# A four-layer decoder trunk: the angles of the position tables on GpSimd, the small vectors on ScalarE's queue, eleven warming products

## The chip, the cores and the metric

The kernel runs on one core of a Trainium2 chip, as one launch. The metric is device microseconds of an execution, the median of several runs. A profile is one execution taken by the hardware profiler; its span goes from the first to the last instruction.

## What is computed

The reference is a trunk of four pre-norm residual layers over 256 tokens of width 1024 in float32. The token mixers are differential attention (layers 0 and 3), block attention (layer 1) and windowed attention with sinks (layer 2); a squared-ReLU MLP of width 4096 follows each. Every mixer rotates the first quarter of each head's width by angles from the token's position:

```python
def rope_tables(positions):
    inv = ROPE_THETA ** (-jnp.arange(0, ROT_DIM, 2, dtype=jnp.float32) / ROT_DIM)
    ang = positions.astype(jnp.float32)[..., None] * inv
    return jnp.cos(ang), jnp.sin(ang)
...
for i in range(DEPTH):
    a = rms_norm(h, attn_norm_g[i])
    y = ...                                    # mixer i % 3, with cos and sin
    h = h + y
    h = h + sqrelu_mlp(rms_norm(h, mlp_norm_g[i]), mlp_w_up[i], mlp_w_down[i])
return rms_norm(h, final_norm_g)
```

Here 8 angles for each of 256 positions are needed, so the tables are 128 x 16 numbers (128 partitions, two token tiles of 8). They are computed once and used by all four layers.

## The kernel before

**Weights.** All weights are cut on the host into pieces of 128 x 2048 floats (1 MB). Each piece is fetched on SP's queue into `raw` (4 buffers), and split into a high part `whi` (ScalarE, L80) and the rest `wlo` (VectorE, L81). A product of float32 precision is then three TensorE products: high by high, high by low, low by high. `take()` keeps fetches and splits ahead of use: two pieces ahead in conversion, five in fetching. The first two pieces are fetched in quarters of 512 columns that alternate with the eight blocks of `x` (L66, L109), and split quarter by quarter; later pieces are split in halves of 1024.

**Norms.** The activations stay transposed in `hT`. `norm_part` (L228, L229) makes the high and low part of the scaled input, `norm_sum` adds squares, `norm_factor` turns the sums into the factor per token (`rsqrt`, L207 to L211, on VectorE with scratch tiles `nw`). The factor is applied behind the projection, by ScalarE, when it copies `qk` out of the accumulator (L588).

**Projection and attention of layer 0.** `proj` runs 48 matmuls of 512 columns for each of six output parts; the first part goes through the weights in the order in which they arrive. `qk` is rotated by `rope` (L304 to L309, VectorE) with `cc`, `sn` and `nsn`, transposed on TensorE (`p_qk`, L461), split, and scored (`p_s`, L271 to L273). The order of these steps among the projections is a list (`plan`).

**The start.** A memset and an activation on ScalarE come first, then the transfer `gn` (L115): norm gains, sub-norm gains and positions in one tile of 34 KB. GpSimd makes constants and masks. TensorE runs `WARM` products of a tile of ones, which are used by nothing.

**The position tables.** `rotary_tables` is a generator. Up to its `yield` it casts the positions, multiplies by the inverse frequencies and takes off the first multiple of a turn; the rest is run when the first projection has been written down. The angle is reduced modulo whole turns in three rounds: the number of turns is rounded by adding and taking off 12582912, and the turn is taken off in four pieces, so that nothing is lost. Then the angle is clamped, its absolute value is taken (L181 to L184), and ScalarE's Sin gives `sn` and `cc` (L185, L186).

**Order.** The kernel is written in a framework that places semaphores by itself and orders each engine's instructions when the program is built, by priority (what was written first) and its own estimate of when operands are ready. On the chip each engine works its queue in that fixed order. So the order in the trace is not that of the text.

Of the kernel before, what the change touches and what calls it, by code (L numbers as in the profile page):

```python
# [11 lines left out]
F32 = mybir.dt.float32  # L12
# [3 lines left out]
OP = mybir.AluOpType  # L16
AX = mybir.AxisListType

P = 128
D = 1024  # L20
S = 256
NT = S // P
# [5 lines left out]
NEG = -1.0e38  # L28
LOOK = 2
FAR = 5  # L30
WARM = 12
RAW = 4


# [5 lines left out]
def trunk(ctx: ExitStack, tc: tile.TileContext, xT, gains, lams, swa_row, fng, weights, out):  # L40
    nc = tc.nc
    V, A, G, T = nc.vector, nc.scalar, nc.gpsimd, nc.tensor

    cst = ctx.enter_context(tc.tile_pool(name="cst", bufs=1))
    tiny = ctx.enter_context(tc.tile_pool(name="tiny", bufs=2))
# [3 lines left out]
    def bank(tag, name):  # L49
        return ps.tile([P, 512], F32, tag=tag, name=name, bufs=4)  # L50
# [50 lines left out]
    gn = cst.tile([P, 2 * DEPTH * 8 + 2 + NT], F32, name="gn")  # L101
    gv = gn[:, :2 * DEPTH * 8].rearrange("p (k l b) -> p k l b", k=2, l=DEPTH)
    sg = gn[:, 2 * DEPTH * 8:2 * DEPTH * 8 + 2]
    posi = gn[:, 2 * DEPTH * 8 + 2:].bitcast(I32)
# [6 lines left out]

    first_act = cst.tile([P, 1], F32, name="first_act")
    V.memset(first_act, 0.0)
    A.activation(first_act, first_act, AF.Copy)
    nc.sync.dma_start(gn, gains)  # L115
    fetch(4, load_x)
    fetch(4, load_x)
    fetch(2)
# [7 lines left out]
    invt = cst.tile([P, NT, 8], F32, name="invt")  # L126
# [4 lines left out]
    warm = bank("wk", "p_warm")  # L131
    for _ in range(WARM):
        T.matmul(warm[:, :P], ones, ones, start=True, stop=True)
# [18 lines left out]
    def rotary_tables():  # L152

        posf = cst.tile([P, NT], F32, name="posf")
        V.tensor_copy(posf, posi)
        an = cst.tile([P, NT, 8], F32, name="an")
        lo = cst.tile([P, NT, 8], F32, name="an_lo")
        V.tensor_tensor(an, invt, posf[:, :, None].to_broadcast([P, NT, 8]), op=OP.mult)
        G.memset(lo, 0.0)

        for turn, bits in ((2.0 ** 16 * math.pi, 10), (2.0 * math.pi, 9), (2.0 * math.pi, 20)):
            q = cst.tile([P, NT, 8], F32, name="turns")
            V.tensor_scalar(q, an, 1.0 / turn, None, op0=OP.mult)
            V.tensor_scalar(q, q, 12582912.0, None, op0=OP.add)
            V.tensor_scalar(q, q, -12582912.0, None, op0=OP.add)
            for x in (an, an, lo):
                m, e = math.frexp(turn)
                c = math.ldexp(math.floor(m * 2 ** bits), e - bits)
                turn -= c
                V.scalar_tensor_tensor(x, q, -c, x, op0=OP.mult, op1=OP.add)  # L170
            if bits == 10:
                yield
            V.scalar_tensor_tensor(lo, q, -turn, lo, op0=OP.mult, op1=OP.add)
            if bits != 20:
                V.tensor_tensor(q, an, lo, op=OP.add)
                V.tensor_tensor(an, an, q, op=OP.subtract)
                V.tensor_tensor(lo, an, lo, op=OP.add)
                V.tensor_copy(an, q)
        V.tensor_tensor(an, an, lo, op=OP.add)
        pi = 3.1415925  # L180
        V.tensor_scalar(an, an, pi, -pi, op0=OP.min, op1=OP.max)  # L181
        ab = cst.tile([P, NT, 8], F32, name="ab")
        V.scalar_tensor_tensor(ab, an, -1.0, an, op0=OP.mult, op1=OP.max)
        V.tensor_scalar(ab, ab, -1.0, math.pi / 2, op0=OP.mult, op1=OP.add)  # L184
        A.activation(sn, an, AF.Sin)  # L185
        A.activation(cc[:, :, 0:8], ab, AF.Sin)  # L186
        V.tensor_copy(cc[:, :, 8:16], cc[:, :, 0:8])
        V.tensor_scalar(nsn, sn, -1.0, None, op0=OP.mult)
# [14 lines left out]

    def rsqrt(y, x, n):

        t = tiny.tile([P, n], F32, tag="nw", name="nw", bufs=7)
        V.tensor_scalar(y.bitcast(I32), x.bitcast(I32), -0.5, 1597463007.0, op0=OP.mult, op1=OP.add)  # L207
        for _ in range(3):
            V.tensor_tensor(t, y, y, op=OP.mult)
            V.scalar_tensor_tensor(t, t, -0.5, x, op0=OP.mult, op1=OP.mult)  # L210
            V.scalar_tensor_tensor(y, t, 1.5, y, op0=OP.add, op1=OP.mult)  # L211
# [483 lines left out]
    def down_out(us, res, factor):  # L695

        grow = sb.tile([P, D], F32, tag="raw", name="grow", bufs=RAW)
        nc.sync.dma_start(grow, bcast(fng, D))
        ss = cst.tile([P, 4, NT], F32, name="fss")
        x = cst.tile([P, 2, NT], F32, name="fx")  # L700
        r = cst.tile([P, NT], F32, name="fr")

        def close(t, p, c, part, first=0):

            width = p.shape[-1]
            y = res[t][:, 512 * c + first:512 * c + first + width]
            V.scalar_tensor_tensor(y, p, factor[:, t:t + 1], y, op0=OP.mult, op1=OP.add)
            if part is not None:
                sq = sb.tile([P, 512], F32, tag="relu", name="sq")
                A.activation(sq[:, :width], y, AF.Square, accum_out=ss[:, part, t:t + 1])  # L710

        def finish(t, halves):

            o = slice(t, t + 1)
            last = x[:, 1, o]
            V.scalar_tensor_tensor(last, ss[:, halves, o], 0.5 / D, x[:, 0, o], op0=OP.mult, op1=OP.add)
            y, w = r[:, o], tiny.tile([P, 1], F32, tag="nw", name="nw", bufs=7)

            V.tensor_scalar(y.bitcast(I32), last.bitcast(I32), -0.5, 1597463007.0 - 2.0 ** 22 - 2.0 ** 31,
                            op0=OP.mult, op1=OP.add)  # L720
            for _ in range(3):
                V.scalar_tensor_tensor(w, y, y, last, op0=OP.mult, op1=OP.mult)
                V.scalar_tensor_tensor(y, w, 1.5, y, op0=OP.subtract, op1=OP.mult)
            rows = slice(P * t, P * t + P)
            A.activation(res[t][:, :512], res[t][:, :512], AF.Copy, scale=y)
            nc.scalar.dma_start(out[rows, :512], res[t][:, :512])
            for z in (slice(512, 768), slice(768, 1024)):
                V.scalar_tensor_tensor(res[t][:, z], res[t][:, z], y, grow[:, z], op0=OP.mult, op1=OP.mult)
                nc.sync.dma_start(out[rows, z], res[t][:, z])

        def sofar(t, parts):
            o = slice(t, t + 1)
            V.tensor_scalar(x[:, 0, o], ss[:, 0, o], 0.5 / D, 0.5 * EPS, op0=OP.mult, op1=OP.add)
            for j in parts:
                V.scalar_tensor_tensor(x[:, 0, o], ss[:, j, o], 0.5 / D, x[:, 0, o], op0=OP.mult, op1=OP.add)

        for c in range(2):
            banks = [bank("acc", "p_last") for _ in range(NT)]
            parts = []

            def last(t, ks, p=None, first=0, alone=False):
                p = banks[t] if p is None else p
                cols = slice(first, first + p.shape[-1])
                for q, k in ks:
                    hi, lo = parts[q]
                    u, s = us[4 * q + k], slice(P * t, P * t + P)
                    mm3(p, u[:, 0, s], u[:, 1, s], hi[:, k, cols], lo[:, k, cols],
                        (q, k) == (ks[0] if alone else (0, 0)), (q, k) == ks[-1] and k == 3 and q > 5,
                        skip_group_check=True)

            for q in range(8):
                parts.append([r3(4)(x) for x in take()])
                if q < 6:
                    for k in range(4):
                        for t in range(NT):
                            last(t, [(q, k)])
            ends = [(q, k) for q in (6, 7) for k in range(4)]
            last(0, ends)
            close(0, banks[0], c, c)
            if c == 0:  # L760
                last(1, ends)
                close(1, banks[1], 0, 0)
                for t in range(NT):
                    y = res[t][:, :512]
                    V.tensor_tensor(y, y, grow[:, :512], op=OP.mult)
                    sofar(t, [])
            else:
                finish(0, 1)

                last(1, ends[:4])  # L770
                close(1, banks[1], 1, None)
                for h in range(2):
                    p = bank("acc", "p_last")[:, :256]
                    last(1, ends[4:], p, 256 * h, True)
                    close(1, p, 1, 1 + h, 256 * h)
                    if h == 0:
                        sofar(1, [1])
                finish(1, 2)
# [3 lines left out]
    n = new_norm(gv[:, 0, 0, :])  # L782
# [5 lines left out]
    for i in range(DEPTH):  # L788
        parts, rest = mixer_layer(i, n)
        n = new_norm(gv[:, 1, i, :])  # L790
# [24 lines left out]
        if i + 1 < DEPTH:  # L815
            n = new_norm(gv[:, 0, i + 1, :])
# [81 lines left out]
```

## Time and profile before

| | |
|---|---|
| Median of 3 runs | 1148.51 us (1148.4 to 1148.52) |
| Profiled execution | 1148.08 us |
| Its span | 1146.0 us |
| Mean granted TensorE clock | 0.998 |
| Busy share of the span | PE 99%, PEld 86%, DVE 72%, ACT 58%, POOL 1% |
| DMA | 198.66 MB, mean 173 GB/s |

PE is TensorE's matmul row, PEld its weight loads, DVE VectorE, ACT ScalarE, POOL GpSimd, SP the engine on whose queue the weights are fetched. A row of a group gives line, engine, operation, output and inputs, shapes and count, then busy time in us and mean ns of one, then the idle time ahead of it and what ended it. A row of the timeline gives start and length in us first. The chain is followed back from the last instruction to what released each step.

### The profile page before, as it was taken

The page shows a single profiled execution, that of the slowest core. Times are in us where ns is not written, and L with a number is a line of the kernel's source. Part 1 is how long each engine was busy: PE and PEld are TensorE (multiplying, and loading weights), DVE is VectorE, ACT ScalarE, POOL GpSimd, SP SyncE. Part 2 cuts the span into 40 slices and gives each one's busy share as a digit, 9 for nine tenths or more (in the row PEclk, how much of TensorE's full clock was granted, in tenths as well). Part 3 has the DMA queues.
Part 4 walks back from the last instruction along what each step waited for, and adds up shares of the span by engine and source line. Part 5 has one row for each costly group of instructions (what it writes and reads, how often), then busy time and mean ns, then how long its engine had stood idle before and what let it go on. Part 6 is the DMA issues. An engine that isn't in the chain of part 4 may idle for free.

```text
span 1146.0 us, 17054 instructions
## 1 busy us (share of the span) xinstructions
PE 1135.6 (99%) x6560; PEld 988.2 (86%) x6560; DVE 827.8 (72%) x1608; ACT 660.0 (58%) x1207; POOL 11.4 (1%) x39
## 2 busy tenths in 40 slices
PE   9999999999999999999999999999999999999997
PEld 7789888888887888888899898888888889888886
DVE  8978977656676698766569887775567788777454
ACT  6866656544476675554446756554447676665342
POOL 1000000000000000000000000000000000000000
PEclk9999999999999999999999999999999999999999
DMA  8543465555543355555563346555554444554551
GB/s 330 195 147 119 167 198 193 198 194 184 184 147 133 125 184 188 190 203 191 185 208 111 111 148 214 190 184 185 187 195 136 148 143 160 191 198 169 184 184 37
DMA packets 30609, 198.66 MB, mean 173 GB/s; under 512 B 3521, under 2 KB 5185, under 8 KB 7361
## 3 DMA queue, kind: packets, MB, share of 16 engines
q1 hardware_dynamic: 30240, 197.06, 50.2%
q8 instruction: 51, 0.84, 0.3%
q10 hardware_dynamic: 288, 0.52, 0.1%
q14 instruction: 30, 0.24, 0.1%
HBM read 196.52 MB, written 1.05 MB: 172 GB/s over the span
## 4 chain that ended last, share of the span: by engine, by line
PE 95%; DVE 2%; DMA 1%; ACT 1%; issue 0%; SPq 0%; DVEq 0%; ACTq 0%
PE p_up L605 20%; PE p_in L296 18%; PE p_down L605 15%; PE p_up L606 11%; PE p_down L606 8%; PE p_last L272 3%; PE p_last L271 3%; PE p_last L273 3%; PE p_d L272 2%; PE p_d L273 2%; PE p_d L271 2%; DMA raw<-in_weights 1%; PE p_t L354 1%; PE p_s L271 1%; PE p_qk L461 1%; PE p_av L436 1%
## 5 line engine op out<-in xcount | busy, mean ns | idle before, releaser
L81 DVE TENSOR_TENSOR wlo<-raw,whi 128x1024 fp32r<-128x1024 f32 (+1 forms) x374 | 447.2, 1209 | 204.1 <-ACT whi L80 203.3
L80 ACT ACTIVATE whi<-raw 128x1024 fp32r<-128x1024 f32 (+1 forms) x374 | 384.3, 1046 | 216.4 <-issue 111.1
L605 PE MATMUL p_up<-hg,whi 128*128 128x512 f32 x1024 | 356.7, 393 | 0.5 <-DVE hg L229 0.2
L606 PE MATMUL p_up<-hg,wlo 128*128 128x256 f32 x1024 | 285.5, 280 | 0.0
L605 PE MATMUL p_down<-uu,whi 128*128 128x512 f32 x768 | 266.4, 391 | 0.0
L605 PEld LDWEIGHTS p_up<-hg,whi 128*128 128x128 f32 x1024 | 191.4, 187 | 42.8 <-DVE hg L229 0.7
L606 PE MATMUL p_down<-uu,wlo 128*128 128x256 f32 x768 | 215.0, 280 | 0.0
L296 PE MATMUL p_in<-whi,hg 128*128 128x512 f32 (+1 forms) x736 | 211.6, 371 | 0.0
L606 PEld LDWEIGHTS p_up<-hg,wlo 128*128 128x128 f32 x1024 | 193.5, 189 | 0.5
L605 PEld LDWEIGHTS p_down<-uu,whi 128*128 128x128 f32 x768 | 143.6, 187 | 31.5
L296 PEld LDWEIGHTS p_in<-whi,hg 128*128 128x128 f32 x736 | 132.2, 189 | 23.3 <-DVE hg L229 0.8
L606 PEld LDWEIGHTS p_down<-uu,wlo 128*128 128x128 f32 x768 | 145.2, 189 | 0.0
L296 PE MATMUL p_in<-wlo,hg 128*128 128x512 f32 (+1 forms) x368 | 130.4, 369 | 0.1
L680 ACT ACTIVATE uu<-u 128x512 fp32r<-128x512 f32 x64 | 40.5, 633 | 71.1 <-DVE u L678 71.1
L296 PEld LDWEIGHTS p_in<-wlo,hg 128*128 128x128 f32 x368 | 68.8, 189 | 12.3 <-DVE wlo L81 1.4
L611 ACT ACTIVATE cross<-p_up 128x256 f32<-128x256 f32 x128 | 47.9, 374 | 39.3 <-PE p_up L606 33.8
L228 ACT ACTIVATE hg<-hT,gn 128x256 fp32r<-128x256 f32 x64 | 31.6, 502 | 65.5 <-DVE hT L624 65.3
L339 ACT ACTIVATE e<-ns,nm 128x128 f32<-128x128 f32 (+1 forms) x128 | 56.8, 446 | 11.6 <-DVE nm L336 11.2
L681 DVE TENSOR_TENSOR uu<-u,uu 128x512 fp32r<-128x512 f32 x64 | 44.2, 691 | 21.4 <-ACT uu L680 21.4
L272 PE MATMUL p_d<-oo,whi 128*128 128x256 f32 x192 | 55.3, 288 | 0.0
L271 PE MATMUL p_d<-oo,whi 128*128 128x256 f32 x192 | 55.2, 288 | 0.0
L612 DVE TENSOR_TENSOR relu<-p_up,cross 128x256 f32<-128x256 f32 x128 | 53.6, 419 | 1.5 <-ACT cross L611 1.5
(182 smaller groups left out, 1247.2 us busy)
## 6 DMA issues: line engine op xcount, KB each, us to landing
raw<-in_weights SPq DMA_DIRECT2D x181, 1024.0 KB, 4.9
raw<-in_weights SPq DMA_DIRECT2D x8, 256.0 KB, 4.6
raw<-in_weights SPq DMA_DIRECT2D x4, 512.0 KB, 6.8
hT<-in_xT SPq DMA_DIRECT2D x8, 128.0 KB, 4.4
bias<-in_swa_row SPq DMA_DIRECT2D x1, 512.0 KB, 4.6
grow<-in_fng SPq DMA_DIRECT2D x1, 512.0 KB, 3.7
out<-res SPq DMA_DIRECT2D x4, 128.0 KB, 2.1
out<-res ACTq DMA_DIRECT2D x2, 256.0 KB, 2.2
```

The lines of the kernel that those rows point to most:

```text
L80: A.activation(hi[:, s], raw[:, s], AF.Copy)
L81: V.tensor_tensor(lo[:, s], raw[:, s], f(hi[:, s]), op=OP.subtract)
L271: T.matmul(out, lh, rh, start=start, stop=False, **kw)
L272: T.matmul(out, lh, rl, start=False, stop=False, **kw)
L273: T.matmul(out, ll, rh, start=False, stop=stop, **kw)
L296: T.matmul(out[t], n.both[k // 2][:, k % 2, x, P * t:P * t + P], r3(kb)(parts[k // kb][w])[:, k % kb, :], start=fresh, stop=k == 7 and x + ...
L339: A.activation(e[:, s], ns[:, s], AF.Exp, bias=nm[:, t:t + 1], scale=-1.0, accum_out=l[:, t:t + 1])
L605: T.matmul(r3(2)(p), hi, x, start=start, stop=False, skip_group_check=True)
L606: T.matmul(p[:, :S], lo, x[:, 0], start=False, stop=stop, skip_group_check=True)
L611: A.activation(cross, p[:, S:], AF.Copy)
L612: V.tensor_tensor(out, p[:, :S], cross, op=OP.add)
L681: V.tensor_tensor(both[:, :, 1], r3(2)(u), f(both[:, :, 0]), op=OP.subtract)
```

## The change

Four edits. The transfer of the small vectors `gn` is issued from ScalarE's queue, ahead of the first activation, instead of first on SP's queue. `WARM` goes from 12 to 11. All of the reduction modulo whole turns, the cast and the product with the frequencies included, goes from VectorE to GpSimd; each fused multiply-add becomes a product into a scratch tile and a sum (`plus`), and the `yield` stands behind the whole reduction instead of inside its first round. The scratch tag `nw` has 13 buffers instead of 7, at both of its places.

```diff
-WARM = 12
+WARM = 11
...
+    nc.scalar.dma_start(gn, gains)
     A.activation(first_act, first_act, AF.Copy)
-    nc.sync.dma_start(gn, gains)
     fetch(4, load_x)
...
         posf = cst.tile([P, NT], F32, name="posf")
-        V.tensor_copy(posf, posi)
+        G.tensor_copy(posf, posi)
         an = cst.tile([P, NT, 8], F32, name="an")
         lo = cst.tile([P, NT, 8], F32, name="an_lo")
-        V.tensor_tensor(an, invt, posf[:, :, None].to_broadcast([P, NT, 8]), op=OP.mult)
+        G.tensor_tensor(an, invt, posf[:, :, None].to_broadcast([P, NT, 8]), op=OP.mult)
         G.memset(lo, 0.0)
+
+        def plus(x, q, c):
+            G.tensor_scalar(w, q, c, None, op0=OP.mult)
+            G.tensor_tensor(x, x, w, op=OP.add)
+
+        w = cst.tile([P, NT, 8], F32, name="an_w")
 
         for turn, bits in ((2.0 ** 16 * math.pi, 10), (2.0 * math.pi, 9), (2.0 * math.pi, 20)):
             q = cst.tile([P, NT, 8], F32, name="turns")
-            V.tensor_scalar(q, an, 1.0 / turn, None, op0=OP.mult)
-            V.tensor_scalar(q, q, 12582912.0, None, op0=OP.add)
-            V.tensor_scalar(q, q, -12582912.0, None, op0=OP.add)
+            G.tensor_scalar(q, an, 1.0 / turn, None, op0=OP.mult)
+            G.tensor_scalar(q, q, 12582912.0, None, op0=OP.add)
+            G.tensor_scalar(q, q, -12582912.0, None, op0=OP.add)
             for x in (an, an, lo):
                 m, e = math.frexp(turn)
                 c = math.ldexp(math.floor(m * 2 ** bits), e - bits)
                 turn -= c
-                V.scalar_tensor_tensor(x, q, -c, x, op0=OP.mult, op1=OP.add)
-            if bits == 10:
-                yield
-            V.scalar_tensor_tensor(lo, q, -turn, lo, op0=OP.mult, op1=OP.add)
+                plus(x, q, -c)
+            plus(lo, q, -turn)
             if bits != 20:
-                V.tensor_tensor(q, an, lo, op=OP.add)
-                V.tensor_tensor(an, an, q, op=OP.subtract)
-                V.tensor_tensor(lo, an, lo, op=OP.add)
-                V.tensor_copy(an, q)
-        V.tensor_tensor(an, an, lo, op=OP.add)
+                G.tensor_tensor(q, an, lo, op=OP.add)
+                G.tensor_tensor(an, an, q, op=OP.subtract)
+                G.tensor_tensor(lo, an, lo, op=OP.add)
+                G.tensor_copy(an, q)
+        G.tensor_tensor(an, an, lo, op=OP.add)
+        yield
         pi = 3.1415925
         V.tensor_scalar(an, an, pi, -pi, op0=OP.min, op1=OP.max)
...
-        t = tiny.tile([P, n], F32, tag="nw", name="nw", bufs=7)
+        t = tiny.tile([P, n], F32, tag="nw", name="nw", bufs=13)
...
-            y, w = r[:, o], tiny.tile([P, 1], F32, tag="nw", name="nw", bufs=7)
+            y, w = r[:, o], tiny.tile([P, 1], F32, tag="nw", name="nw", bufs=13)
```

## The prediction

> **What bounds the kernel now.** I read the page first, then the chain that ended last in order of time, then the matmul groups and waits of the first 45 us.
>
> ```profile
> span 1146.0 us, 17054 instructions
> PE 95%; DVE 2%; DMA 1%; ACT 1%; issue 0%; SPq 0%; DVEq 0%; ACTq 0%
> ```
>
> TensorE holds 95% of the chain. What is left lies mostly in the first 36 us, and all that the change touches runs there. So the question is how many microseconds TensorE loses before it settles. The chain there (start, length, what):
>
> ```profile
> 0.75 0.39 SPq L115
> 1.13 0.06 issue
> ...
> 11.02 7.12 DMA raw<-in_weights
> ...
> 18.21 1.07 ACT whi L80
> ...
> 22.35 0.08 DVE an L170
> ...
> 26.54 1.28 ACT L185
> ...
> 28.43 0.19 DVE ropeb L307
> ...
> 29.24 1.04 issue
> 30.28 0.43 DVE qk L309
> ...
> 53.12 2.73 PE p_in L296 x12
> ```
>
> The first link is the issue of the small vectors (L115) ahead of the weights on SP's queue. Then the DMA sets the time until 18.1 us, then VectorE with pieces of the position tables (L170) between its conversions, then the Sin table load (L185), then the first rotation (L307 to L309). The last row gives TensorE's rate: 2.73/12 = 0.2275 us for a 512-wide matmul.
>
> ```profile
> L296 PE MATMUL p_in<-whi,hg 128*128 128x512 f32 x33 | 10.1, 391 | 0.0
> L296 PE MATMUL p_in<-wlo,hg 128*128 128x512 f32 x18 | 7.3, 415 | 0.1
> ...
> PEld p_in L296 <- DVE wlo L81: 1.4, 4, 0.5
> PE p_qk L461 <- DVE qk L309: 0.7, 1, 0.7
> PE p_s L271 <- issue: 0.6, 1, 0.6
> ```
>
> The first two rows are the groups from 17.6 to 30.7 us: 33 + 18 = 51 matmuls, worth 51 x 0.2275 = 11.6 us, in 13.1. The last three are the waits up to 45 us: 1.4 us on late `wlo` halves, 0.7 on the first rotated `qk`, 0.6 ahead of the first scores. The waits are 2.7 us in total; that is nearly all there is to win behind the start. The stages (width, then PE, PEld, DVE, ACT, POOL busy, clock, DMA share):
>
> ```profile
> 6.00:7.00 1.00, 1.00 (x7) 0.87 (x6) 0.53 (x2) 0.93 (x2) 0.00 (x0) 1.00 0.96 334
> ...
> 20.00:22.00 2.00, 2.00 (x10) 1.38 (x9) 2.00 (x8) 0.50 (x1) 0.00 (x0) 1.00 0.96 401
> 22.00:24.00 2.00, 2.00 (x10) 1.32 (x9) 2.00 (x10) 0.00 (x0) 0.00 (x0) 1.00 1.11 438
> ...
> 28.00:30.00 2.00, 2.00 (x10) 1.49 (x8) 1.82 (x6) 2.00 (x5) 0.00 (x0) 1.00 0.23 94
> ```
>
> From 20 to 24 us VectorE is full, ScalarE all but idle and GpSimd empty; at 28 ScalarE is the full one. The granted clock is 1.00 throughout.
>
> **The change, part by part.** The sums are made against the profiled execution, 1148.08 us (span 1146.0 and 2.08 around it); the median of the runs is 1148.51, 0.43 above it, so I subtract the same gain from the median.
>
> *Small vectors on ACT's queue, eleven warming products.*
>
> ```profile
> 4.51 0.63 ACT L80 ACTIVATE whi<-raw 128x512 fp32r<-128x512 f32 x1 [2.27 <-DMA raw<-in_weights]
> 1.00 5.27 PE L133 MATMUL p_warm<-ones 128*128 128x128 f32 x24 [1.00 <-POOL ones L124]
> 5.05 0.49 ACT L228 ACTIVATE hg<-hT,gn 128x256 fp32r<-128x256 f32 x1
> 6.03 1.17 PE L296 MATMUL p_in<-whi,hg 128*128 128x512 f32 x4
> 2.48 0.45 DVE L155 CAST posf<-gn 128x2 f32<-128x2 int32 x1 [1.61 <-DMA gn<-in_gains]
> ```
>
> SP's queue loses 0.39 + 0.06 = 0.45 us ahead of the first weights, and every issue behind it moves up by that. The DMA share is 0.96 and more soon after, so the landings move up by the same. One warming product is two of the 24 pieces, 5.27 x 2/24 = 0.44 us. The two belong together: the first operand `hg` is there at 5.05 + 0.49 = 5.54, but the warm products hold TensorE until the first projection starts at 6.03. With one less, it can start at 5.59; the data would then be there at 5.1. Gain 0.44 us. On ACT the issue stands before the activation at L114; ScalarE's first conversion ran at 4.51 after 2.27 us of idle time, so an issue of about 0.4 us is covered. `gn` itself lands no later than at 2.48 plus what it loses among the weight packets; `hg` wants it 2 us later. Bound of the pair: 0 (if the DMA gives the 0.45 back) to 0.45; I take 0.44, since the chain runs through it.
>
> *The angles on GpSimd.* VectorE loses one cast, one product, 9 scalings, 12 fused multiply-adds, 8 steps of the two renormalisations and the last sum: 32 instructions. The last three (clamp and absolute value, L181 to L184) stay. GpSimd gets 44, since each of the 12 fused ones becomes a product and a sum. They hang on each other in one chain.
>
> ```profile
> 10.47 0.17 DVE L170 SCALAR_TENSOR_TENSOR an_lo<-turns,an_lo 128x16 f32<-128x16 f32 x1
> 16.35 0.17 DVE L173 SCALAR_TENSOR_TENSOR an_lo<-turns,an_lo 128x16 f32<-128x16 f32 x1
> 24.30 1.27 ACT L588 ACTIVATE qk<-p_in,nr 128x512 f32<-128x512 f32 x2 [3.80 <-DVE an L176]
> 26.52 0.17 DVE L184 TENSOR_SCALAR ab<-ab 128x16 f32<-128x16 f32 x1
> ...
> L81 DVE TENSOR_TENSOR wlo<-raw,whi 128x1024 fp32r<-128x1024 f32 x7 | 8.6, 1222 | 0.3 <-ACT whi L80 0.3
> L210 DVE SCALAR_TENSOR_TENSOR nw<-nw,nx 128x2 f32<-128x2 f32 x3 | 0.5, 154 | 0.0
> L242 DVE TENSOR_TENSOR acc<-acc 128x256 f32<-128x256 f32 x1 | 0.4, 425 | 0.0
> ```
>
> The instructions before 4.4 us lie in VectorE's wait for the first weights and cost nothing. The bulk starts at 16.35. From there to the end of the row norm, which releases `qk` at 24.30 - about 7.9 us - VectorE must do four halves of 1.222 us, one sum of 0.425 and 11 small norm steps of about 0.155: 4.89 + 0.43 + 1.71 = 7.0 us. The table steps put in between (14, by the timeline) thus cost 0.85 us net, not 14 x 0.17 = 2.4; most fill the gaps between dependent norm steps. I count 0.85 of the 1.4 us wait on `wlo` as won. It cannot be all: the halves still follow their DMA landings.
>
> ScalarE waited 3.80 us for the norm, then scaled `qk`, converted, loaded the Sin table (1.28 us at 26.54, the clamp and absolute value having ended at 26.69) and only then was the rotation possible. If the angles are finished well before 24 us, table load and both Sin lie in ScalarE's idle stretch and the rotation can follow the scaling of `qk` directly, at about 25.5 instead of 28.4. That is nearly 3 us of lead over TensorE's waits of 0.7 at `p_qk` and 0.6 at `p_s`, so both go: 1.3 us.
>
> Sum: 0.44 + 0.85 + 1.3 = 2.6 us. 1148.08 - 2.6 = 1145.5 for the profiled execution, 1145.9 for the median. At most 0.45 + 2.7 = 3.2 us can be won here, 1145.3; behind 36 us TensorE runs without a wait over 0.3 us for a long while. What is late next is the conversion on ScalarE, full at 28 us.
>
> *Two slots become more* for `nw` (7 to 13): nothing moves; at most 14 are ever asked for.
>
> *What does a step on GpSimd cost?* No row shows arithmetic there. The nearest:
>
> ```profile
> L139 POOL TENSOR_SCALAR_AFFINE_SELECT band<-band 128x128 f32<-128x128 f32 x2 | 0.6, 305 | 0.1
> L159 POOL MEMSET an_lo<- 128x16 f32 x1 | 0.1, 112 | 0.0
> ```
>
> A memset of the same 16 columns takes 0.112 us, a select over eight times the columns 0.305. I take 0.2 for a dependent step, between the two. From about 2.9 us: 44 x 0.2 = 8.8 us, ending near 11.7; the ends are 44 x 0.112 = 4.9 (7.8) and 44 x 0.305 = 13.4 (16.3). All lie before 16.35, where VectorE had turned to the rest.
>
> The Trainium skill, "GPSIMD Engine Reference", 4.1 Engine selection, speaks against the move: elementwise work belongs on VectorE, two-input operations being about twice as slow on GpSimd. No run here shows that yet; by it, with 0.17 us of the rows above, 20 two-input steps at 0.34 and 24 at 0.17 give an estimated 10.9 us, which would end at 13.8 and leave the sum as it is.
>
> **Rivals.**
>
> *R1, hidden anyway (no lead).* The order in each queue is fixed when the program is built. If Sin still stands behind the scaling of `qk` and a conversion on ScalarE, the rotation gains little and `p_qk` waits as before. The row at 10.47 speaks for it: written ahead of all conversions, it ran behind most of those of the first projection, so steps are not put where the data would allow. Gain then 0.44 to 0.44 + 0.85: 1148.1 to 1147.2, 1147.6 in the middle.
>
> *R2, VectorE stands behind GpSimd.* The clamp (L181) now waits for GpSimd, and behind it in VectorE's queue are the `wlo` halves, for which TensorE waits already. If the clamp stands where the rest of the tables did (16.35) and the chain is not done, all that is queued behind it stops. It decides at (16.35 - 2.9)/44 = 0.31 us a step. That is the slow end above, and steps could be slower still if each has to wait for VectorE to finish an operation. VectorE starts one every 0.6 us from 5.2 to 17.3: the 16 of these rows and four sums.
>
> ```profile
> L81 DVE TENSOR_TENSOR wlo<-raw,whi 128x512 fp32r<-128x512 f32 x8 | 5.5, 688 | 1.8 <-ACT whi L80 1.8
> L229 DVE SCALAR_TENSOR_TENSOR hg<-hT,gn,hg 128x256 fp32r<-128x256 f32 x8 | 3.8, 479 | 0.0
> ```
>
> If GpSimd gets in one step for each, (5.2 - 2.9)/0.2 = 11 are done by 5.2 and (16.35 - 5.2)/0.6 = 18 more by 16.35; 15 at 0.2 us remain, a stop of 3.0 us. Less the start of 0.44: 1151.1.
>
> *R3, the two engines hold each other up.*
>
> ```profile
> 2.97 0.52 POOL L369 MEMSET kpadh<- 64x512 f32 x1
> 3.25 0.27 DVE L163 TENSOR_SCALAR turns<-an 128x16 f32<-128x16 f32 x1
> 3.56 0.17 DVE L164 TENSOR_SCALAR turns<-turns 128x16 f32<-128x16 f32 x1
> ```
>
> L163 took 0.27 us instead of 0.17, ending at 3.52, just behind the memset's 3.49: it looks held until the memset ended. If each GpSimd step holds VectorE for 0.112 us where VectorE is the bound, that is up to 44 x 0.112 = 4.9 us on it, less the 0.85 and the 0.44: +3.6, 1152.1; with half the steps in gaps, 1149.7. Against it: no larger operation of VectorE is seen stretched. The Trainium skill, "SBUF - State Buffer", "Who interferes with whom", has this as a rule: one pair of ports is shared under an exclusive lock, taken by a two-input VectorE operation against a GpSimd one that reads. The L163 row agrees with such a lock; for two-input operations no run here shows it.
>
> **How the numbers follow.** The forecast has 0.52, of which 0.42 gains over 0.2% (2.3 us, about what a measurement of this kernel can tell from no change) and 0.10 falls just short, the sum of 2.6 being so near that bound. R1 0.15, within 0.2%. R2 0.22 and R3 0.11, slower. So faster 0.42, same 0.25, slower 0.33. The range reaches from the most that can be won and a little that a new order may add, 1144.8, to the dear end of R3, 1152.1. The forecast's own range is 1145.3 to 1147.0.
>
> **What would show it.** Right: the first `p_in` at about 5.6 us; GpSimd's last step before 16 us; the Sin load at 20 to 24 us inside ScalarE's idle time; no wait of TensorE on L309 near 30 us; VectorE's halves as long as before. Wrong: VectorE idle before L181 with GpSimd as its releaser (R2), `wlo` rows longer than 1.22 us or GpSimd steps of 0.5 us and more (R3), the Sin load still behind the scaling of `qk` (R1). A gain or loss that lies behind 40 us would mean that the order of later work changed, which nothing here prices.

## The result and the profile after

The median of after is 1155.43 us (six runs, 1154.78 to 1155.8) against 1148.51 us for before (six runs): a ratio of 1.0059 with a 95% interval of 1.0048 to 1.0069. The kernel became 6.9 us slower. The forecast was 1145.9 us with a range up to 1152.1. The profiled execution took 1155.45 us, its span 1153.7.

The page of after, span, busy time and the chain's share by engine:

```profile
span 1153.7 us, 17061 instructions
PE 1137.1 (99%) x6558; PEld 987.5 (86%) x6558; DVE 823.4 (71%) x1576; ACT 659.9 (57%) x1207; POOL 26.5 (2%) x83
PE 96%; POOL 2%; DVE 1%; issue 0%; DMA 0%; ACT 0%; DVEq 0%; POOLq 0%
```

Two per cent of the chain are now GpSimd's: 18 us of its steps, with 3.4 us of issue between them. The waits of the first 45 us (total, times, longest):

```profile
DVE an L186 <- POOL an L183: 8.0, 1, 8.0
...
PE p_in L301 <- DVE wlo L81: 7.2, 1, 7.2
ACT sn L190 <- DVE an L186: 7.0, 1, 7.0
```

The first row is rival R2 as it was written down: the clamp (L186 after the change) stands in VectorE's queue and waits for GpSimd; the `wlo` halves queued behind it stop, and TensorE waits 7.2 us for one of them. The waits on `p_qk` and `p_s` that before had are gone. The timeline of after at that place, VectorE, ScalarE and TensorE:

```profile
16.77 1.23 DVE L81 TENSOR_TENSOR wlo<-raw,whi 128x1024 fp32r<-128x1024 f32 x1
17.91 0.15 DVE L256 TENSOR_SCALAR nx<-p_sum 128x2 f32<-128x2 f32 x1
26.10 0.17 DVE L186 TENSOR_SCALAR an<-an 128x16 f32<-128x16 f32 x1 [8.03 <-POOL an L183]
...
18.04 1.28 ACT L190 ACT_TABLE_LOAD   x1
26.30 0.22 ACT L190 ACTIVATE sn<-an 128x16 f32<-128x16 f32 x1 [6.98 <-DVE an L186]
...
27.74 0.79 PE L301 MATMUL p_in<-wlo,hg 128*128 128x512 f32 x1 [7.20 <-DVE wlo L81]
```

All of it lies at the start. The rows of the first up-projections, before and after (shortest, median and longest in ns, then first and last start):

```profile
L605 PE MATMUL p_up<-hg,whi x1024: 389/391/586, 119.2 to 1051.1; 128*128 128x512 f32 x171
L610 PE MATMUL p_up<-hg,whi x1024: 387/391/586, 126.6 to 1058.7; 128*128 128x512 f32 x171
```

The first `p_up` of layer 0 starts 7.4 us later, the last one of layer 3 7.6 us later. GpSimd's chain:

```profile
4.63 0.18 POOL L155 CAST posf<-gn 128x2 f32<-128x2 int32 x1 [1.78 <-DMA gn<-in_gains]
...
8.35 0.78 POOL L170 TENSOR_SCALAR turns<-turns 128x16 f32<-128x16 f32 x1
9.08 0.52 POOL L374 MEMSET kpadl<- 64x512 f32 x1
...
16.98 1.13 POOL L170 TENSOR_SCALAR turns<-turns 128x16 f32<-128x16 f32 x1
18.20 0.25 POOL L171 TENSOR_SCALAR turns<-turns 128x16 f32<-128x16 f32 x1
18.53 0.26 POOL L162 TENSOR_SCALAR an_w<-turns 128x16 f32<-128x16 f32 x1
...
25.84 0.22 POOL L183 TENSOR_TENSOR an<-an,an_lo 128x16 f32<-128x16 f32 x1
```

It reads in two parts. From 18.20 us VectorE stands still: 25 steps, the last starting at 25.84, so (25.84 - 18.20)/24 = 0.318 us from step to step. Ahead of that VectorE works: 19 steps between 4.63 and 18.20, less 3.3 us for GpSimd's other work there (five memsets and the selects of `band`), which is 10.3/19 = 0.54 us a step. The row at 16.98 took 1.13 us, where the same operation takes 0.26 with VectorE idle (at 22.60); VectorE ran a conversion of 1024 columns from 16.77 to 18.00.

### The profile page after: what moved, and what is told of

Same layout as the page of the kernel before. It is cut to its first block, busy times and chain, and to the rows that moved or that the text cites. A ratio compares the mean times of both kernels' runs of the same rounds, so it can differ in the third digit from the quotient of the medians.

```text
span 1153.7 us, 17061 instructions
## 1 busy us (share of the span) xinstructions
PE 1137.1 (99%) x6558; PEld 987.5 (86%) x6558; DVE 823.4 (71%) x1576; ACT 659.9 (57%) x1207; POOL 26.5 (2%) x83
## 4 chain that ended last, share of the span: by engine, by line
PE 96%; POOL 2%; DVE 1%; issue 0%; DMA 0%; ACT 0%; DVEq 0%; POOLq 0%
PE p_up L610 20%; PE p_in L301 19%; PE p_down L610 15%; PE p_up L611 10%; PE p_down L611 8%; PE p_last L278 3%; PE p_last L277 3%; PE p_last L276 3%; PE p_d L277 2%; PE p_d L278 2%; PE p_d L276 2%; PE p_t L359 1%; PE p_s L276 1%; PE p_qk L466 1%; PE p_av L441 1%; PE p_s L277 1%
```

## Experiments

All times are medians, and the ratio to before is given with its 95% interval. The unchanged kernel before gave 1148.54 to 1148.85 us beside them.

**1. The load and the warming product alone.** On before:

```diff
-WARM = 12
+WARM = 11
+    nc.scalar.dma_start(gn, gains)
     A.activation(first_act, first_act, AF.Copy)
-    nc.sync.dma_start(gn, gains)
```

> The kernel before with the small vectors on ACT's queue and 11 warming products, the angles on VectorE as before. Theory: the start gains 0.1 to 0.4 us (first projection at 5.5 instead of 6.0 us, but the first weights landed only 0.1 us earlier), 1148.1 to 1148.4 us. Rival (the start is the loss): 1151 us or more.

Measured: 1148.38 us, 0.9998 [0.9989, 1.0008]. The start is not the loss, and alone it is no gain. From VectorE and TensorE of this run:

```profile
4.24 0.60 DVE L155 CAST posf<-gn 128x2 f32<-128x2 int32 x1 [3.36 <-DMA gn<-in_gains]
...
6.32 0.69 DVE L81 TENSOR_TENSOR wlo<-raw,whi 128x512 fp32r<-128x512 f32 x1
...
7.54 0.74 PE L296 MATMUL p_in<-whi,hg 128*128 128x512 f32 x2 [1.66 <-DVE hg L229]
```

The vector lands later on ACT's queue (3.5 us from issue to landing instead of 1.7 on SP's), the first piece of the angles on VectorE starts at 4.24 instead of 2.48 and stands ahead of the first `wlo`, and TensorE waits 1.66 us. Some of these pieces also last longer beside GpSimd's memsets:

```profile
4.87 1.08 POOL L369 MEMSET kpadl<- 64x512 f32 x2
5.46 0.52 DVE L164 TENSOR_SCALAR turns<-turns 128x16 f32<-128x16 f32 x1
```

L164 took 0.17 us in before and takes 0.52 here; it ends at 5.98, just behind the second memset's 5.95. So alone, with the angles on VectorE, the load on ACT's queue gives back at the first `wlo` what it gains ahead of it.

**2. The angles alone.** On after:

```diff
-WARM = 11
+WARM = 12
-    nc.scalar.dma_start(gn, gains)
     A.activation(first_act, first_act, AF.Copy)
+    nc.sync.dma_start(gn, gains)
...
-        t = tiny.tile([P, n], F32, tag="nw", name="nw", bufs=13)
+        t = tiny.tile([P, n], F32, tag="nw", name="nw", bufs=7)
```

> The kernel after with the small vectors back on SP's queue, 12 warming products and 7 buffers: the angles on GpSimd alone. Theory (VectorE's queue stands at the clamp until GpSimd's chain of 44 steps ends): the chain starts near 2.5 us instead of 4.6 and ends near 23 to 24, but the clamp now stands one conversion earlier in VectorE's queue, so TensorE stands idle from about 17.5 us for 6 to 7 us: 1154 to 1155.5 us. Rival (the late small vectors and the colder start are the loss): 1148.5 to 1149 us.

Measured: 1165.15 us, 1.0145 [1.013, 1.016], 10 us above the theory's expectation and 16 above the rival's. At the start the theory holds: the chain runs from 2.81 to 23.2 us, VectorE waits 6.5 us at the clamp, and the first `p_up` starts at 126.8, as late as that of after. The other 10 us lie behind it: from the first to the last `p_up` are 941.8 us instead of 931.9 in before, and TensorE waits no longer there (0.2 us in both). The matmuls themselves take longer. Experiment 5 follows that.

**3. Where the clamp stands.** After, with the clamp and what follows it held behind the last step of the norm factor in VectorE's queue:

```diff
-                    next(tables, None)
+                    with tc.issue_after(marks[0]):   # marks[0]: last step of rsqrt
+                        next(tables, None)
```

> The kernel after, with the clamp and what follows it held in VectorE's queue behind the last step of the row norm; GpSimd's steps are the same. Theory: TensorE's wait of 7.2 us near 20 us goes; GpSimd ends later, near 28 to 29 us, because VectorE now works beside it; TensorE then waits 1 to 3 us for the first rotated qk: 1148.5 to 1150.5 us. Rival (the loss lies in the new order of later work, or in GpSimd's steps as such): stays over 1153 us.

Measured: 1152.42 us, 1.0035 [1.0021, 1.005], outside both expectations. The 7.2 us wait on `wlo` is gone, as the theory has it, but a wait of 5.0 us on the rotation takes its place instead of 1 to 3: the rotation needs the tables, and GpSimd's chain now ends later. GpSimd and VectorE of this run:

```profile
18.64 0.22 POOL L163 TENSOR_TENSOR an<-an,an_w 128x16 f32<-128x16 f32 x1
18.95 1.22 POOL L162 TENSOR_SCALAR an_w<-turns 128x16 f32<-128x16 f32 x1
20.25 0.22 POOL L163 TENSOR_TENSOR an<-an,an_w 128x16 f32<-128x16 f32 x1
20.56 1.21 POOL L162 TENSOR_SCALAR an_w<-turns 128x16 f32<-128x16 f32 x1
...
18.82 1.23 DVE L81 TENSOR_TENSOR wlo<-raw,whi 128x1024 fp32r<-128x1024 f32 x1
...
20.43 1.22 DVE L81 TENSOR_TENSOR wlo<-raw,whi 128x1024 fp32r<-128x1024 f32 x1
...
PE p_qk L469 <- DVE qk L317: 5.0, 1, 5.0
```

A step that starts 0.13 us behind a conversion ends 0.12 us behind that conversion's end; the next one, which falls into the small norm steps, takes 0.22 us. So GpSimd gets two steps into 1.6 us. VectorE's conversions keep their 1.22 us: GpSimd alone loses. The chain ends at 28.8 us instead of 26.1.

**4. A shorter chain.** After without the third round of the reduction (11 steps fewer; that round of the reduction is left out), the clamp held at its place behind `nx`:

```diff
-        for turn, bits in ((2.0 ** 16 * math.pi, 10), (2.0 * math.pi, 9), (2.0 * math.pi, 20)):
+        for turn, bits in ((2.0 ** 16 * math.pi, 10), (2.0 * math.pi, 9)):
```

> The kernel after without the third round of the reduction (left out: the last 11 of 44 steps and the angles' last digits), the clamp held at the same place in VectorE's queue as in the kernel after. Theory: 11 steps of 0.32 us less, the chain ends at 22.5 us instead of 26.1, VectorE stands 4.5 us instead of 8.0 and TensorE 3.7 instead of 7.2: 1151.5 to 1152 us, and down to 1150.5 us if the shorter wait leaves TensorE's clock at full speed. Rival (the length of the chain does not matter): 1155 us.

Measured: 1151.43 us, 1.003 [1.0019, 1.004]. The chain ends at 22.1 us, 4.0 earlier than in after: 11 x 0.318 is 3.5, and the vector landed early enough in this run for the chain to start at 4.08 us instead of 4.63. VectorE waits 3.4 us at the clamp instead of 8.0, and the time falls by 4.0 us. What the chain ends earlier here, the kernel gains.

**5. Seven or thirteen buffers.** After with seven buffers, and before with thirteen. In both the instructions and their order on each engine are the same as without the edit; what changes is where the tiles lie in SBUF that are placed behind the small ones (`raw`, `whi`, `wlo`, `hg`, `uu` and others). The build gives each small buffer 32 bytes, so six more move them up by 192; the new scratch tile `an_w` moves them by 64. Two further runs move them in before by unused floats behind a small tile:

```diff
-    nlam = cst.tile([P, 2], F32, name="nlam")
+    nlam = cst.tile([P, 2 + 16], F32, name="nlam")[:, :2]    # 64 bytes; 2 + 32 for 128 bytes
```

> The kernel after with seven buffers for nw again: every instruction stays as it was, in the same order on every engine, and all tiles placed behind the small ones in SBUF stand 192 bytes lower, 64 bytes above their places in the kernel before. Theory (the seven buffers put weights and activations at places at which the 512-wide matmuls of the MLPs take 399 ns instead of 391, as in the run of the angles alone): 1155.4 + 10 = about 1165.5 us, with the same start as after. Rival (the longer matmuls came from the gains vector on SP or the twelfth warming product, or from the order that followed): 1155.4 us.

> The kernel before with thirteen buffers for nw and nothing else: the instructions and their order stay, and the tiles behind move up by 192 bytes. Theory of the places, in units of 256 bytes: 192 is as bad as 64, MLP matmuls at about 399 ns, 1148.5 + 10 = 1158.5 us. Theory of the places where only +64 is bad: 1148.5 us. Rival of the prediction (the buffers move nothing): 1148.5 us with matmuls at 391 to 392 ns.

> The kernel before with 128 unused bytes behind the two lambdas: the instructions and their order stay, and the tiles behind move up by 128 bytes. If what counts is the place modulo 128 bytes: 1148.5 us. If modulo 256: about 1158 us, or something between. If places do not count at all: 1148.5 us, and then the run with 64 or 192 bytes shows none either.

> The kernel before with 64 unused bytes behind the two lambdas: instructions and order stay, the tiles behind move up by 64 bytes. Theory (the place alone costs 10 us): matmuls of the MLPs at 399 ns and about 1158.5 us. Rival (64 bytes hurt only together with the other work of after): 1148.5 us.

| Kernel | Tiles above before's | Time, us | Ratio to before |
|---|---|---|---|
| after | 256 bytes | 1155.43 | 1.0059 [1.0048, 1.0069] |
| after, seven buffers | 64 bytes | 1165.47 | 1.0148 [1.0132, 1.0163] |
| before, 64 unused bytes | 64 bytes | 1156.46 | 1.0071 [1.0056, 1.0086] |
| before, 128 unused bytes | 128 bytes | 1151.87 | 1.0026 [1.0017, 1.0036] |
| before, thirteen buffers | 192 bytes | 1148.56 | 1.0001 [0.9991, 1.001] |

The groups of the MLP's matmuls between 130 and 900 us, after with seven buffers, then before, then before with 64 bytes:

```profile
L610 PE MATMUL p_down<-uu,whi 128*128 128x512 f32 x768 | 271.5, 399 | 0.0
L610 PE MATMUL p_up<-hg,whi 128*128 128x512 f32 x765 | 270.9, 399 | 0.2 <-DVE hg L234 0.2
```

```profile
L605 PE MATMUL p_down<-uu,whi 128*128 128x512 f32 x768 | 266.4, 391 | 0.0
L605 PE MATMUL p_up<-hg,whi 128*128 128x512 f32 x744 | 259.0, 392 | 0.2 <-DVE hg L229 0.2
```

```profile
L605 PE MATMUL p_down<-uu,whi 128*128 128x512 f32 x768 | 269.8, 396 | 0.0
L605 PE MATMUL p_up<-hg,whi 128*128 128x512 f32 x746 | 262.7, 397 | 0.2 <-DVE hg L229 0.2
```

The same matmuls in the same order take 391, 396 or 399 ns by where the tiles lie, at a granted clock of 1.00 in all three. That the place counts holds, in after and in before; that 192 bytes are as bad as 64 falls, and so does the prediction's "nothing moves", by the runs with 64 and 128. The size is not one number, though: 64 bytes cost 10.0 us in after and 7.9 in before, 128 cost 3.3 (in nine of ten runs; one took 1148.61 us), 192 nothing. Which tile's place counts, and why only the MLPs of layers 0 to 2 feel it (in layer 3 all of these run at 391 ns), was not tried and stays open. So the thirteen buffers are no idle edit: without them the change costs 16.9 us instead of 6.9.

**6. The later landing.** After with the vector back on SP's queue and twelve warming products, but thirteen buffers, so that the tiles stay where after has them. The clamp is held behind `nx`, its place in after, in the first run, and behind the norm factor in the second.

> After with the gains vector back on SP and twelve warming products, with the thirteen buffers (so that the tiles stand where after's stand) and the clamp held behind nx, its place in after. The clean undo of the part about the load. Theory (the later landing of the gains vector, 4.6 instead of 2.8 us, let GpSimd's chain end later and is part of the loss): the chain ends near 23.5 us instead of 26.1 and the time is about 1153 us. Rival (the run of the angles alone lost as much as after up to the first p_up, so the load has no part in it): 1155.4 us.

> The same, but with the clamp held behind the last step of the norm factor. Theory (the loss is the end of GpSimd's chain against the place of the clamp): the chain, 28.8 us in the run with the clamp held behind, ends near 26.8 us; the wait at the clamp falls from 5.3 to about 3.3 us and the time from 1152.4 to about 1150.4 us. Rival (the chain is held up by VectorE's conversions whenever it starts, and gives the head start back): 1152.4 us.

Measured: 1153.56 us, 1.0045 [1.0029, 1.006], and 1151.16 us, 1.0021 [1.0012, 1.003]. In the first the chain starts at 2.79 instead of 4.63 us and ends at 24.1 instead of 26.1; VectorE's wait:

```profile
DVE an L186 <- POOL an L183: 5.7, 1, 5.7
PE p_in L304 <- DVE wlo L81: 5.3, 1, 5.3
```

A chain that starts 1.8 us earlier ends 2.0 us earlier and gives 1.9 us back (2.2, when each kernel is set against the before measured beside it): of the 6.9 us that is the part of the load and the warming product together. With the clamp held back as well, the chain ends at 27.0 instead of 28.8 us, TensorE waits 3.2 instead of 5.0, and 1.3 us are won, between the expectations of 2.0 and 0. Even so placed, the angles on GpSimd cost more than they save.

**7. The change with its cost taken out.** After with no round of the reduction (the angles stay unreduced), and after with all 44 steps replaced by memsets of the same tiles (the angles are left out):

```diff
-        for turn, bits in ((2.0 ** 16 * math.pi, 10), (2.0 * math.pi, 9), (2.0 * math.pi, 20)):
+        for turn, bits in ():
```

```diff
-            G.tensor_scalar(w, q, c, None, op0=OP.mult)
-            G.tensor_tensor(x, x, w, op=OP.add)
+            G.memset(w, 0.5)
+            G.memset(x, 0.5)
```

> After with the three rounds of the reduction left out (the angles stay unreduced; only the conversion, the product and one addition stay on GpSimd), so that GpSimd's chain costs next to nothing; its tiles stand 192 bytes above before's, a place that cost nothing in the run of the buffers alone. This is the change with its cost taken out, and so the most that it can gain. If the prediction's terms of gain were right: 1148.5 - 0.1 (start as measured) - 0.85 - 0.9 (Sin load as measured) = about 1146.7 us. If what VectorE is relieved of was hidden already (rival R1): 1147.5 us. Theory that GpSimd's chain is the whole loss: anything below 1148.5 us bears it out; 1150 us or more would show a second cause in the start.

> After with each of the 44 steps on GpSimd replaced by a memset of the same tile (the angles are left out); the steps depend on one another as before but read nothing. Theory (a step is stretched beside VectorE because it cannot read its operands while a two-input operation of VectorE holds the port): no step stretches beyond about 0.35 us beside VectorE, and the chain of 44 ends near 4.6 + 44 x 0.3 + 3 for the other work of GpSimd = 20 us or earlier. Rival (GpSimd is held up whatever it does, writes too): steps of 0.5 to 1.2 us remain beside the conversions, and the chain ends near 26 us as in after. Here the three VectorE steps stand earlier in the queue, so the time of the whole says little.

Measured: 1147.74 us, 0.9996 [0.9987, 1.0005]; and one run of 1146.56 us against 1148.54. The clamp stands earlier in VectorE's queue in both. Neither is slower than before (the interval of the first leaves room for 0.6 us at most), so GpSimd's chain is the whole loss. Of the expectations the first lies next to 1147.5 us, by which VectorE's relief was hidden already. TensorE has no wait on `p_qk` or `p_s` in either, and the first `p_up` starts at 118.1 and 117.7 us instead of 119.2: by these rows the change without its cost wins 1.1 to 1.5 us at the start, not 2.6 (0.8 us by the median of the first, which is within the noise).

The second run also shows which steps VectorE holds up. Its memsets run 0.045 us apart and do not wait for one another, so it is no longer a chain, and its end, near 8 us, says nothing of a chain's. But 24 of the 44 fall beside a two-input operation of VectorE, and neither they nor that operation last longer:

```profile
5.11 0.10 POOL L171 MEMSET turns<- 128x16 f32 x1
5.15 0.10 POOL L163 MEMSET an<- 128x16 f32 x1
5.20 0.11 POOL L162 MEMSET an_w<- 128x16 f32 x1
...
4.77 0.69 DVE L81 TENSOR_TENSOR wlo<-raw,whi 128x512 fp32r<-128x512 f32 x1 [0.27 <-ACT whi L80]
```

The Trainium skill, "SBUF — State Buffer", "Who interferes with whom", has it that a VectorE instruction with two SBUF inputs contends with a GpSimd instruction that reads SBUF, and not with one that only writes. Both halves agree with these rows: 1.22 us for reading steps beside a conversion in experiment 3, 0.10 to 0.11 for memsets here.

**8. The Sin table early, without GpSimd.** On before, with the angles left on VectorE: one Sin of a single element on ScalarE right behind the last conversion of the first staged weights, so that the table load runs in the idle stretch. The second run has the edit of experiment 1 as well.

```diff
+                    with tc.issue_after(split[0]):   # split[0]: last conversion to whi so far
+                        A.activation(first_act, first_act, AF.Sin)
                     next(tables, None)
```

> The kernel before with one added Sin of a single element on ScalarE right behind the last conversion of the first staged weights, so that the 1.28 us load of the Sin table lies in ScalarE's idle stretch instead of ahead of the scaling of q and k. This is the prediction's term of 1.3 us taken alone. If that term was right: waits of TensorE on p_qk and p_s gone, 1147.2 us. If the waits have another cause that is late next (rival R1 of the prediction in this one term): 1148.5 us.

> The kernel before with the early load of the Sin table (1147.7 us alone) and with the gains vector on the ACT queue and eleven warming products (1148.4 us alone); the angles stay on VectorE. If the two gains add up: 1147.68 - 0.1 = about 1147.5 us. If the later landing of the gains vector delays the angles on VectorE, so that the scaling of q waits for them again: 1148 us or more.

Measured: 1147.68 us, 0.999 [0.9981, 0.9999], and 1147.23 us, 0.9985 [0.9977, 0.9994]. ScalarE in the first:

```profile
21.36 1.28 ACT L582 ACT_TABLE_LOAD   x1
22.65 0.20 ACT L582 ACTIVATE first_act<-first_act 128x1 f32<-128x1 f32 x1
24.39 1.27 ACT L591 ACTIVATE qk<-p_in,nr 128x512 f32<-128x512 f32 x2 [1.54 <-DVE an L177]
25.55 1.06 ACT L80 ACTIVATE whi<-raw 128x1024 fp32r<-128x1024 f32 x1
26.49 0.21 ACT L186 ACTIVATE sn<-an 128x16 f32<-128x16 f32 x1
```

The load lies in what was a wait of 3.80 us, and `sn` comes at 26.49 instead of 27.83. TensorE's waits on `p_qk` and `p_s` fall from 0.7 and 0.6 to 0.2 and none. That is the term of 1.3 us, measured at 0.9. Its interval reaches from 0.1 to 2.2 us, but the first `p_up` agrees, at 118.3 instead of 119.2. The second is the fastest kernel of this study that computes the whole, and its time lies below both expectations: beside the early Sin load, the edit of experiment 1 gave 0.45 us by the medians, though only 0.2 by the first `p_up`.

**9. The lower clock behind the gap.** In after the granted clock, in stretches of 2 us, was 0.68 from 24 to 26 us, 0.50 from 26 to 30, 0.61 from 30 to 32, and 1.00 from then on. In finer stretches it is two steps: 1.00 until 24.7 us, 0.50 until 31.5, and 1.00 again. After with 32 more warming products in the queue ahead of the matmul that waits:

```diff
+            if fill and at == 7:
+                with tc.issue_after(mm):
+                    for _ in range(fill):
+                        mm = T.matmul(warm[:, :P], ones, ones, start=True, stop=True)
```

> After with 32 more warming products in TensorE's queue right ahead of the matmul that waited 7.2 us, so that TensorE is busy through the gap while everything else, the gap's length too, stays. If the lower clock behind the gap (0.50 for 4 us, 0.61 for 2 us) costs what it seems to, some 1 to 1.7 us: 1153.7 to 1154.4 us. If the stretch behind the gap is bound by VectorE catching up and not by TensorE's clock: 1155.4 us.

Measured: 1157.38 us, 1.0078 [1.0061, 1.0094]: neither. The clock stayed at 1.00 through the gap and behind it, but the order of the attention's steps changed with the added work: TensorE comes to `p_qk` 17 matmuls behind the gap instead of 26, and waits 1.6 us for it, which after does not. So the time of the run does not tell what the clock costs. The rows ahead of `p_qk` do in part, after first, then this run:

```profile
28.33 1.05 PE L301 MATMUL p_in<-whi,hg 128*128 128x512 f32 x2
28.12 0.62 PE L307 MATMUL p_in<-whi,hg 128*128 128x512 f32 x2
```

At 0.50 these matmuls start 0.43 us apart, at 1.00 0.23. The 17th behind the gap starts 5.53 us after the first in after (27.74 to 33.27) and 4.69 us in this run (27.78 to 32.47, its own waits included). That is an estimate of 0.8 us for the clock. Another estimate bounds it from above: with the first `p_up` of the run without rounds at 118.1, after lost 126.6 - 118.1 = 8.5 us, of which 7.2 is the wait; 1.3 us are left for the clock and all else.

## Why the prediction was wrong

**The step that failed is the price and the end of the chain on GpSimd.** The prediction took 0.2 us a step, from 2.9 us, and so an end at 11.7; its dear end was 0.305 us and 16.3. The chain ended at 26.1. By the rows of after, 4.63 (start) + 3.3 (GpSimd's other work) + 19 x 0.54 + 25 x 0.318 = 26.1. Against the prediction:

- The price alone. A dependent step of 16 columns takes 0.318 us from start to start, above the dear end of the bounds; the 44 take 14.0 us even alone, where the prediction has 8.8. Its second estimate, 10.9 us, was too low as well. The select of 128 columns, the row taken for the dear end, was no upper bound: with an eighth of its columns a step still lasts 0.20 to 0.26 us. Also, the durations of rows were taken, and not the distance of two dependent starts.
- The price beside VectorE. 0.54 us, since a step that falls beside a two-input operation of VectorE ends only behind it. The prediction had that in R2, as one step for each operation, and priced the stop at 3.0 us; it was 8.0, because the other points came on top.
- The start. It was "no later than 2.48 plus what it loses among the weight packets", and that loss was taken as small. It was 2 us (experiment 6: 1.9 us of the time).
- Not counted: GpSimd's own memsets and selects, which stand among the steps, 3.3 us.

**R2 is what happened**, with 0.22 given to it. Its path was right: the clamp waits, and the `wlo` halves behind it. Its point of decision, 0.31 us a step from 2.9 to 16.35, was too generous: the chain started at 4.63, 3.3 us of other work stood in it, and the clamp could have run at 18.06, so (18.06 - 4.63 - 3.3)/44 = 0.23 us a step was all there was room for. A step's 0.318 alone is beyond both. Experiments 3, 4, 6 and 7 show it from four sides: moving the clamp back, shortening the chain, starting it earlier and taking it out each give time back. R3 had one of its signs come true, GpSimd steps of 0.5 us and more, but not its price: beside them the `wlo` halves of 1024 columns kept 1.22 to 1.23 us (experiment 3). GpSimd is held, and VectorE loses only by waiting for the chain's end. Where VectorE is held by GpSimd, as in its row of L163 and in L164 in experiment 1, it is a small one-input step beside a memset, and the change takes these steps off VectorE.

**The terms of the gain.** The early Sin load: right in kind, 0.9 us instead of 1.3. The start: 0.44 expected; in after the first `p_in` came at 5.51 instead of 6.03 us and `p_sum` at 16.8 instead of 17.2. But the landings did not move up by 0.45 us as assumed (the first conversion of ScalarE starts at 4.43 instead of 4.51), and alone the edit gave 0.1, for the reason in experiment 1. VectorE's relief, 0.85 expected: by the first `p_up`, 119.2 - 118.1 or 117.7, less 0.9 and 0.1, is 0.1 to 0.5 us. The rows of before allowed less than 0.85, too: of the 7.95 us from 16.35 to 24.30, less the 7.02 of necessary work, 0.34 is VectorE's wait for `whi` ahead of the conversion at 19.34, which leaves 0.6. All gains together were 1.1 to 1.5 us instead of 2.6.

**"Nothing moves" for the thirteen buffers** was wrong. No instruction moves, but the tiles do, and 64 bytes cost 7.9 to 10.0 us where no wait shows them. It was luck that 64 of `an_w` and 192 of the buffers made 256, at which nothing shows.

## What to carry to other kernels

Before moving a chain of small dependent steps to an idle engine, price it by the distance of dependent starts on that engine, beside the neighbour that it will run next to, and add what already stands in its queue; an empty row in the profile is no price. Then look at what waits for its end in a fixed queue: the consumer's place counts beside the chain's length, since all that is queued behind it stops too (here 3.0 us came back by moving the consumer, 4.0 by leaving out a quarter of the chain). If a time changes with no new wait in the trace, compare the busy time of the same groups of matmuls, and where their tiles lie.

## What was not expected of the hardware

- GpSimd's small dependent steps cost 0.318 us from start to start where VectorE's of the same shape start 0.21 us apart (3.56 and 3.77 us in before), and last 1.09 to 1.22 us beside a conversion of 1024 columns, which itself stays at 1.22 to 1.23.
- The other way round, a small one-input step of VectorE lasted 0.52 us instead of 0.17 beside GpSimd's memsets of 512 columns (L164, experiment 1).
- The place of tiles in SBUF, by 64 or 128 bytes, changes the mean of a 512-wide matmul from 391 to 399 ns and the kernel by up to 10 us. At 256 bytes nothing showed; at 192 the 512-wide ones took 394 and the 256-wide 277 instead of 280, with no change in the time, so the mean of one group alone can mislead.
- In after the granted clock fell from 1.00 to 0.50 at 24.7 us, 4.2 us after the last matmul had ended, and full speed came back 3.8 us after work did. A gap of 2.9 us was enough for the same: in experiment 4 TensorE stood from 20.86 to 23.76 us, and the clock fell to 0.50 at 24.7 us, with matmuls running again, for 3.4 us.
- The same 34 KB took 3.3 to 3.8 us from issue to landing on ACT's queue beside the weights, and 1.7 to 1.9 us on SP's queue ahead of them.
